# Low-rank products of a token-shift layer fed by the tokens, with two scaled sets of weights

## The chip, the cores and the metric

The kernel runs on one core of a Trainium2 chip. The metric is the device time of one execution in microseconds, from the first to the last instruction and the little around them; lower is better. Five engines share the work: PE (matrix products, with PEld for its weight loads), DVE and ACT (elementwise work, also on the accumulators of PE), POOL (elementwise work outside the accumulators) and SP, whose queue issues nearly all transfers.

## What is computed

The program is a network of three layers over 512 tokens of 1024 features, with a second stream of 256 context tokens in the first two. The change lies in layer 1, an RWKV layer. Its features start from a shift of every token to its neighbours:

```
def centred_shift(x):
    prev = jnp.pad(x[:, :-1], ((0, 0), (1, 0), (0, 0)))
    nxt = jnp.pad(x[:, 1:], ((0, 0), (0, 1), (0, 0)))
    return 0.5 * (prev + nxt) - x

def rwkv_features(h, mu, wr, wk, wv, w0, w1, w2, a0, a1, a2, g1, g2, ...):
    xx = centred_shift(h)
    mix = lambda j: h + xx * mu[j]
    xw, xk, xv, xa = mix(1), mix(2), mix(3), mix(4)
    k = xk @ wk
    v = heads(xv @ wv)
    for d in range(2):
        w_raw = heads(w0[d] + jnp.tanh(xw @ w1[d]) @ w2[d])
        a = jax.nn.sigmoid(heads(a0[d] + (xa @ a1[d]) @ a2[d]))
    r = heads(mix(0) @ wr)
    g = jax.nn.sigmoid(mix(5) @ g1) @ g2
```

`h` are the normalised and modulated tokens. Three pairs of weights are low-rank: `w1, w2` (decay), `a1, a2` and `g1, g2` (gate), with 128 inner features each once both directions `d` stand side by side. The products with `w1`, `a1`, `g1` are called the first low-rank products here, those with `w2`, `a2`, `g2` the second ones. All is fp32; the big products are split into a rounded part and a rest and done in three matmuls, the first low-rank products are done in plain fp32.

## The kernel before

Features lie on the 128 partitions (8 blocks of 128), tokens along the free axis. `features` (L1325) does the stage in question, in this order of the program:

- The six halves `lw` of the first low-rank weights are loaded (L1336) into slots of the tag `mixh`, of which there are nine.
- Layer 0's last residual sums and norms run (`residual` L688, `rms_bc` L641). For the three groups (context, first and second half of the tokens) `modulate` (L673) then makes `h` in fp32: DVE scales by the norm (L678), ACT adds the shift (L680) into `hc` (context) and `hx` (tokens), which have a zero column on either side. POOL adds the two neighbours of each token (L1352) and DVE makes `xc` and `xx` of it (L1353).
- `lora` (L1376) does a first low-rank product: for each of 8 feature blocks DVE mixes `h + xx * mu` into `mix_t` (L1382), and one matmul (L1383) accumulates it. Decay (`u` 0) and a (`u` 1) do context, then tokens in parts of 255 and 257; the gate (`u` 2) does 512 tokens at once, and comes later.
- `evac_dir` (L1386) takes the result out on ACT, turned round for the second direction, and `split` (L1390) splits it into `lr_hi` and `lr_lo`.
- `lora2` (L1395) does a second low-rank product: 16 heads, each three matmuls for 512 and three for 256 columns, an ACT tanh of each (L1405, `lr_out`), and a store. `w2bd` comes first, then the gate's first product, `a2bd`, the mixing of the operand of `wk` (`mix` L1362: DVE L1369, a cast on ACT and a subtraction on DVE in `split_sb` L594, into slots `mixh` and `mixl`), and `gates` (L1413).
- `proj` (L1460) does the product with `wk` in four units of 256 columns, each with `evac_k` (L1476) behind it: squares, norms over PE (L1487, L627) and copies turned round by POOL. Then `wr` in the same way, then `wv` together with the beginning of the scan (`Scan`, `front(0)`).

PSUM is divided into four banks `mm`, three `st` and one `a` (L1360). `st` and `a` lie where the norms of the three groups (`s0` to `s2`) lay. The order on each engine is not the program's own: a scheduler takes the instructions of the program and lays them out per engine by its own estimate of when operands are ready. An engine then does them strictly in that order. Weights of 256 columns are loaded, cast on ACT (L583, `wh`) and subtracted on DVE (L584, `wl`), two at a time (`wsplit` L578).

```
        lora2("w2bd", ts[0], hw[:, 0], self.sd, True)
        ps = self.pt("mm")
        lora(5, 2, ("x", 0, NX), ps)
...
        lora2("a2bd", ts[1], hw[:, 1], self.td, False)
        first = lambda j, wname, groups: (self.wsplit(self.i[wname][0]), mix(j, groups))
        wk = first(2, "wk", both)
        gates(tg)
...
        proj(wk, "wk", both, evac_k)
...
        proj(first(0, "wr", xo), "wr", xo, evac_r)
```

## Time and profile before

| | |
|---|---|
| median of three runs | 3165.51 us (3158.48 to 3166.71) |
| the profiled execution's own time | 3160.86 us |
| its span | 3158.9 us |
| PE busy | 2820.4 us (89%) |
| DVE busy | 1789.2 us (57%) |
| ACT busy | 1551.0 us (49%) |
| POOL busy | 1140.5 us (36%) |
| mean granted clock of PE | 0.927 of 2.4 GHz |

The table's shares are means over the whole span. The stage of the change takes some 230 us of it, from about 980 us (last norms of layer 0) to about 1210 us (begin of the product with `wr`), so it has to be read from rows of that stretch: the busy time of each engine in windows, the order of instructions in time, and what ended each wait. A granted clock of 0.50 is 1.2 GHz, 1.00 is 2.4 GHz. An fp32 matmul appears in the trace as two records, one of a split product as one.

### The profile page before, as it was taken

How to read it: one execution, taken by the hardware profiler on the slowest of the kernel's cores; microseconds unless marked ns; L12 is line 12 of the kernel's file. 1: busy time of each engine (PE TensorE's matmuls, PEld its weight loads, DVE VectorE, ACT ScalarE, POOL GpSimd, SP SyncE). 2: the span in 40 equal slices, each digit the busy share in tenths (PEclk: the TensorE clock that was granted, in tenths of full speed). 3: DMA queues.
4: the chain of work that ended last, by engine and by line, in shares of the span. 5: the costliest groups of instructions: out<-in, count | busy, mean ns of one | idle time of the engine just before them, and what ended most of it. 6: DMA issues, size and time to landing. Idle time of an engine off the chain costs nothing.

```text
span 3158.9 us, 50961 instructions
## 1 busy us (share of the span) xinstructions
PE 2820.4 (89%) x19290; PEld 2338.0 (74%) x19290; DVE 1789.2 (57%) x3558; ACT 1551.0 (49%) x3103; POOL 1140.5 (36%) x1500
## 2 busy tenths in 40 slices
PE   6999879999996899887777779699997999989999
PEld 6967778888885687764666667587776885678887
DVE  8466383444448725758688742644446654555364
ACT  3247556666664633554566532455543444544341
POOL 4013446667665212045666640256543210010000
PEclk9999989999998999987688889899998995999999
DMA  5323213333331465432233231255441220022322
GB/s 225 125 86 101 101 64 117 127 114 131 118 106 72 187 196 149 167 118 84 81 95 106 83 117 50 99 175 183 169 146 54 81 94 1 15 79 90 104 98 83
DMA packets 138115, 346.72 MB, mean 110 GB/s; under 512 B 16400, under 2 KB 48784, under 8 KB 120592
## 3 DMA queue, kind: packets, MB, share of 16 engines
q1 hardware_dynamic: 137872, 343.48, 31.8%
q8 instruction: 152, 2.49, 0.3%
q14 instruction: 91, 0.75, 0.1%
HBM read 294.40 MB, written 49.02 MB: 109 GB/s over the span
## 4 chain that ended last, share of the span: by engine, by line
PE 32%; DVE 8%; ACT 6%; POOL 6%; DMA 4%; issue 2%; SPq 0%; ACTq 0%; POOLq 0%; DVEq 0%
PE mm L590 7%; PE mm L591 7%; PE mm L592 6%; POOL acc L733 3%; DMA adaw<-in_ada_dram 3%; ACT wh L583 1%; PE st L1247 1%; PE a L329 1%; PE a L1290 1%; POOL M L428 1%; POOL Mt L427 1%; PE y L520 1%; ACT adat L732 1%; PE b L1241 1%; PE a L1924 1%
## 5 line engine op out<-in xcount | busy, mean ns | idle before, releaser
L733 POOL TENSOR_TENSOR acc<-acc,adat 128x256 f32<-128x256 f32 x658 | 575.8, 898 | 529.5 <-ACT acc L729 427.7
L584 DVE TENSOR_TENSOR wl<-wr,wh 128x2048 fp32r<-128x2048 f32 (+3 forms) x145 | 317.7, 2191 | 367.1 <-ACT wh L583 364.6
L732 ACT ACTIVATE adat<-adaw,silu 128x256 f32<-128x256 f32 x644 | 319.1, 508 | 262.1 <-POOL acc L733 161.2
L583 ACT CAST wh<-wr 128x2048 fp32r<-128x2048 f32 (+2 forms) x147 | 266.6, 1814 | 232.0 <-PE mm L591 218.1
L590 PE MATMUL mm<-fh,wh 128*128 128x512 f32 (+1 forms) x1008 | 347.3, 353 | 16.1 <-DVE relu L1015 11.7
L591 PE MATMUL mm<-fl,wh 128*128 128x512 f32 (+1 forms) x1008 | 350.8, 350 | 0.0
L592 PE MATMUL mm<-fh,wl 128*128 128x512 f32 (+1 forms) x1008 | 349.8, 349 | 0.9 <-DVE wl L584 0.9
L590 PE MATMUL mm<-h_xhi,wh 128*128 128x512 f32 (+1 forms) x784 | 278.5, 360 | 3.3 <-ACT h_xhi L596 1.9
L591 PE MATMUL mm<-h_xlo,wh 128*128 128x512 f32 (+1 forms) x784 | 277.9, 357 | 1.8 <-DVE h_xlo L686 1.5
L592 PE MATMUL mm<-h_xhi,wl 128*128 128x512 f32 (+1 forms) x784 | 277.8, 356 | 0.0
L664 POOL TENSOR_TENSOR acc<-acc,t 128x256 f32<-128x256 f32 x127 | 109.0, 866 | 345.5 <-ACT t L662 342.6
L590 PEld LDWEIGHTS mm<-fh,wh 128*128 128x128 f32 x1008 | 190.0, 189 | 43.8 <-DVE relu L1015 14.0
L592 PEld LDWEIGHTS mm<-fh,wl 128*128 128x128 f32 x1008 | 190.6, 189 | 25.5 <-DVE wl L584 1.1
L591 PEld LDWEIGHTS mm<-fl,wh 128*128 128x128 f32 x1008 | 190.7, 189 | 25.3 <-DVE fl L597 2.2
L1039 DVE TENSOR_TENSOR y<-mm,y 128x512 f32<-128x512 f32 (+1 forms) x184 | 99.2, 559 | 141.9 <-PE mm L592 141.4
L590 PE MATMUL mm<-h_hi,wh 128*128 128x512 f32 (+1 forms) x408 | 160.8, 398 | 6.7 <-ACT h_hi L685 6.7
L590 PEld LDWEIGHTS mm<-h_xhi,wh 128*128 128x128 f32 x784 | 148.0, 191 | 23.1 <-ACT h_xhi L596 2.1
L592 PEld LDWEIGHTS mm<-h_xhi,wl 128*128 128x128 f32 x784 | 148.9, 190 | 21.4 <-issue 0.2
L591 PEld LDWEIGHTS mm<-h_xlo,wh 128*128 128x128 f32 x784 | 148.9, 191 | 20.7 <-DVE h_xlo L686 1.7
L427 POOL TENSOR_TENSOR Mt<-M 128x30 f32<-128x30 f32 (+14 forms) x240 | 141.0, 588 | 56.3 <-PE f L443 21.8
L591 PE MATMUL mm<-h_lo,wh 128*128 128x512 f32 (+1 forms) x408 | 160.4, 394 | 0.0
L592 PE MATMUL mm<-h_hi,wl 128*128 128x512 f32 (+1 forms) x408 | 159.5, 393 | 0.0
(451 smaller groups left out, 6932.4 us busy)
## 6 DMA issues: line engine op xcount, KB each, us to landing
adaw<-in_ada_dram SPq DMA_DIRECT2D x256, 256.0 KB, 2.7
wr<-in_w_dram SPq DMA_DIRECT2D x64, 1024.0 KB, 4.9
wr<-in_wup_dram SPq DMA_DIRECT2D x22, 1024.0 KB, 4.8
base<-b SPq DMA_DIRECT2D x32, 384.0 KB, 3.2
ZU<-vt SPq DMA_DIRECT2D x192, 64.0 KB, 2.5
wr<-in_wdn_dram SPq DMA_DIRECT2D x16, 704.0 KB, 4.0
wr<-in_win_dram SPq DMA_DIRECT2D x9, 1024.0 KB, 4.7
wr<-in_evin_dram SPq DMA_DIRECT2D x8, 1024.0 KB, 4.8
```

Source lines behind the costliest of these rows:

```text
L329: nc.tensor.matmul(ps[:, c], bk[g][:, c0 + c].rearrange("p a t -> p (a t)"), G[:, :na, c0 + c, :], start=True, stop=True)
L427: nc.gpsimd.tensor_tensor(t, a, b, ALU.mult)
L428: nc.gpsimd.tensor_tensor(M[:, s + 1:, :s], M[:, s + 1:, :s], t, ALU.add)
L583: nc.scalar.copy(hi[:, :n], raw[:, :n])
L584: (eng or nc.vector).tensor_tensor(lo[:, :n], raw[:, :n], hi[:, :n], ALU.subtract)
L590: mm(out, lhs[0], rhs[0], start=first, stop=False)
L591: mm(out, lhs[0], rhs[1], start=False, stop=False)
L592: return mm(out, lhs[1], rhs[0], start=False, stop=last)
L664: nc.gpsimd.tensor_tensor(acc, acc, sq, ALU.add)
L732: nc.scalar.activation(t, w, AF.Copy, scale=s)
L733: nc.gpsimd.tensor_tensor(acc, acc, t, ALU.add)
L1039: nc.vector.tensor_tensor(yb, ps[:, :n], yb, ALU.add)
```

## The change

The mix is linear, so `(h + xx * mu) @ W` is `h @ ((1 - mu) W) + (left + right neighbour of h) @ (mu/2 W)`, and the second product can be made of `h` itself and its result moved by one token to either side. The change does this for the three first low-rank products.

- After the load of `lw`, two DVE instructions make `1 - mu` and `mu / 2` (`omu`), and 48 ACT instructions of 128x128 make two scaled sets of weights: `lws` (new, in six of the nine slots `mixl`) and `lw` scaled in place.
- `lora` has no mixing on DVE. For each feature block it does two matmuls on `h`, one into `pn` (scale `mu / 2`) and one into `ps` (scale `1 - mu`). The token parts are 256 and 256. `pn` takes two banks `st` for decay, one `st` and `a` for a, and one `st` for the gate.
- `both_sides` puts a result together: POOL sets two columns to zero, ACT copies `pn` into SBUF, and DVE adds it to `ps` twice, moved by one token each way. `evac_dir` reads that sum.
- The second product `a2bd` and `gates` stand behind the product with `wk` in the program, no longer ahead of it.

`xc` and `xx` are still made: the operands of `wk`, `wr` and `wv` are mixed as before.

```diff
--- before.py
+++ after.py
@@ -1334,6 +1334,16 @@
         for u in range(3):
             for k in range(2):
                 nc.sync.dma_start(lw[u * 2 + k][:, :512], self.i["lora1"][u, :, k * 512:(k + 1) * 512])
+
+        omu = mp.tile([128, 2, 48], F32, name="omu")
+        nc.vector.tensor_scalar(omu[:, 0], self.col("mu", 0, 48), -1.0, 1.0, ALU.mult, ALU.add)
+        nc.vector.tensor_scalar(omu[:, 1], self.col("mu", 0, 48), 0.5, None, ALU.mult)
+        lws = [[mp.tile([128, NT], F32, name="lws", tag="mixl", bufs=8 + 1) for _ in range(6)], lw]
+        for u, j in enumerate((1, 4, 5)):
+            for k in range(8):
+                s, f = slice(k % 4 * 128, k % 4 * 128 + 128), u * 2 + k // 4
+                nc.scalar.activation(lws[0][f][:, s], lw[f][:, s], AF.Copy, scale=omu[:, 0, j * 8 + k:j * 8 + k + 1])
+                nc.scalar.activation(lw[f][:, s], lw[f][:, s], AF.Copy, scale=omu[:, 1, j * 8 + k:j * 8 + k + 1])
         for t, n in ((hx, NX), (hc, NC_)):
             nc.gpsimd.memset(t[:, :, 0:1], 0.0)
             nc.gpsimd.memset(t[:, :, n + 1:n + 2], 0.0)
@@ -1373,19 +1383,30 @@
 
         both, xo = self.groups(), (("x", 0, NX, 0),)
 
-        def lora(j, u, part, ps):
+        def lora(j, u, part, ps, pn):
 
             g, o, n = part
-            h, d = (hc, xc) if g == "c" else (hx, xx)
+            h = hc if g == "c" else hx
             for i in range(8):
-                t = self.tmp.tile([128, 512], F32, name="mix_t", tag="t")
-                nc.vector.scalar_tensor_tensor(t[:, :n], d[:, i, o:o + n], self.col("mu", j * 8 + i), h[:, i, o + 1:o + n + 1], ALU.mult, ALU.add)
-                nc.tensor.matmul(ps[:, o:o + n], lw[u * 2 + i // 4][:, i % 4 * 128:i % 4 * 128 + 128], t[:, :n], start=i == 0, stop=i == 7)
-
-
-        def evac_dir(dst, ps, o, n, func):
-            nc.scalar.activation(dst[0:64, o:o + n], ps[0:64, :n], func)
-            nc.scalar.activation(dst[64:128, o:o + n][:, ::-1], ps[64:128, :n], func)
+                s, f = slice(i % 4 * 128, i % 4 * 128 + 128), i // 4
+                for p, q in ((pn, 1), (ps, 0)):
+                    nc.tensor.matmul(p[:, o:o + n], lws[q][u * 2 + f][:, s], h[:, i, o + 1:o + n + 1], start=i == 0, stop=i == 7)
+
+        def both_sides(ps, pn, n, t, o):
+
+            b = self.tmp.tile([128, 516], F32, name="lr_n", tag="lr_n", bufs=2)
+            nc.gpsimd.memset(b[:, 0:1], 0.0)
+            nc.gpsimd.memset(b[:, n + 1:n + 2], 0.0)
+            nc.scalar.copy(b[:, 1:n + 1], pn[:, :n])
+            nc.vector.tensor_tensor(t[:, o:o + n], ps[:, :n], b[:, 0:n], ALU.add)
+            nc.vector.tensor_tensor(t[:, o:o + n], t[:, o:o + n], b[:, 2:n + 2], ALU.add)
+
+
+        def evac_dir(dst, ps, pn, o, n, func):
+            t = self.tmp.tile([128, 512], F32, name="lr_s", tag="t")
+            both_sides(ps, pn, n, t, 0)
+            nc.scalar.activation(dst[0:64, o:o + n], t[0:64, :n], func)
+            nc.scalar.activation(dst[64:128, o:o + n][:, ::-1], t[64:128, :n], func)
 
         def split(t, n):
             hi, lo = (lp.tile([128, NT], F32R, name=k, tag=k, bufs=2) for k in ("lr_hi", "lr_lo"))
@@ -1422,27 +1443,27 @@
                 nc.sync.dma_start(self.gd[s, :], u[:, :NX])
 
         both_lora = ((1, 0, AF.Tanh), (4, 1, AF.Copy))
-        pss = [(self.pt("mm"), self.pt("mm")) for _ in both_lora]
-        for part in parts:
+        pss = [[self.pt(t) for t in tags] for tags in (("mm", "mm", "st", "st"), ("mm", "mm", "st", "a"))]
+        for part in (("c", 0, NC_), ("x", 0, 256), ("x", 256, 256)):
             for (j, u, _), ps in zip(both_lora, pss):
-                lora(j, u, part, ps[part[0] == "x"])
+                x = part[0] == "x"
+                lora(j, u, part, ps[x], ps[2 + x])
         ts = []
         for (_, _, func), ps in zip(both_lora, pss):
             t = p2.tile([128, NT], F32, name="lr", tag="rev")
-            evac_dir(t, ps[0], 0, NC_, func)
-            evac_dir(t, ps[1], NC_, NX, func)
+            evac_dir(t, ps[0], ps[2], 0, NC_, func)
+            evac_dir(t, ps[1], ps[3], NC_, NX, func)
             ts.append(split(t, NT))
         lora2("w2bd", ts[0], hw[:, 0], self.sd, True)
-        ps = self.pt("mm")
-        lora(5, 2, ("x", 0, NX), ps)
+        ps, pn = self.pt("mm"), self.pt("st")
+        lora(5, 2, ("x", 0, NX), ps, pn)
         t = p2.tile([128, NT], F32, name="lr", tag="rev")
-        nc.scalar.activation(t[:, :NX], ps, AF.Tanh, scale=0.5)
+        both_sides(ps, pn, NX, t, 0)
+        nc.scalar.activation(t[:, :NX], t[:, :NX], AF.Tanh, scale=0.5)
         nc.vector.tensor_scalar(t[:, :NX], t[:, :NX], 0.5, 0.5, ALU.mult, ALU.add)
         tg = split(t, NX)
-        lora2("a2bd", ts[1], hw[:, 1], self.td, False)
         first = lambda j, wname, groups: (self.wsplit(self.i[wname][0]), mix(j, groups))
         wk = first(2, "wk", both)
-        gates(tg)
 
         def rev(src, n, b, fwd, bwd):
 
@@ -1495,6 +1516,8 @@
             rev(kk, NT, b, self.b0, self.b1)
 
         proj(wk, "wk", both, evac_k)
+        lora2("a2bd", ts[1], hw[:, 1], self.td, False)
+        gates(tg)
 
         def evac_r(b, pss):
             t = p2.tile([128, NT], F32, name="rblk", tag="kblk")
```

On ACT, in the last norms of layer 0, ahead of the first `hc`. `acc` and `t` are the squares of `rms_bc` (L649 and L662), `lws` and `lw` the two sets of weights. Before:

```order
L662 ACTIVATE acc<-x 128x256
L649 ACTIVATE t<-y 128x256 x2
L608 ACTIVATE rs_t<-rms_v 128x2
L662 ACTIVATE t<-x 128x256
L653 ACTIVATE t<-t 128x256
L662 ACTIVATE t<-x 128x256 x6
L649 ACTIVATE t<-x 128x256 x2
L608 ACTIVATE rs_t<-rms_v 128x2
```

In the changed kernel:

```order
L662 ACTIVATE acc<-x 128x256
L1345 ACTIVATE lws<-lw,omu 128x128 x2
L649 ACTIVATE t<-y 128x256
L1345 ACTIVATE lws<-lw,omu 128x128 x2
L1346 ACTIVATE lw<-lw,omu 128x128
L649 ACTIVATE t<-y 128x256
L1345 ACTIVATE lws<-lw,omu 128x128 x2
L1346 ACTIVATE lw<-lw,omu 128x128
L1345 ACTIVATE lws<-lw,omu 128x128 x2
L1346 ACTIVATE lw<-lw,omu 128x128
L1345 ACTIVATE lws<-lw,omu 128x128 x4
L1346 ACTIVATE lw<-lw,omu 128x128
```

All 48 scalings stand between the squares of the norms, ahead of the first `hc`.

On ACT, in the second product `w2bd`. `lr_out` is the tanh of a head, `mixh` the cast of the operand of `wk`. Before (the rows alternate like this for all of `w2bd`):

```order
L1405 ACTIVATE lr_out<-mm,hw 128x256
L1405 ACTIVATE lr_out<-mm,hw 128x512
L583 CAST wh<-wr 128x2048
L1405 ACTIVATE lr_out<-mm,hw 128x256
L1405 ACTIVATE lr_out<-mm,hw 128x512
```

In the changed kernel:

```order
L1400 COPY lr_n<-st 128x512
L596 CAST mixh<-mix_t 128x512
L1426 ACTIVATE lr_out<-mm,hw 128x512
L1426 ACTIVATE lr_out<-mm,hw 128x256
L596 CAST mixh<-mix_t 128x256
L1426 ACTIVATE lr_out<-mm,hw 128x512
L1426 ACTIVATE lr_out<-mm,hw 128x256
L596 CAST mixh<-mix_t 128x512
L596 CAST mixh<-mix_t 128x256
```

The casts of `wk`'s operand, which stood between the heads of `a2bd`, now stand between those of `w2bd`.

On PE, at the end of the product with `wk`. `st<-cst,rb` and `st<-cst,sq` are the norms of `evac_k`, `lr_hi` and `lr_lo` the operand of a second low-rank product. Before:

```order
L592 MATMUL mm<-mixh,wl 128x512
L1487 MATMUL st<-cst,sq 128x2 x4
L627 MATMUL st<-cst,rb 128x128 x6
L1487 MATMUL st<-cst,sq 128x2 x6
L627 MATMUL st<-cst,rb 128x128 x6
L590 MATMUL mm<-mixh,wh 128x512 x4
```

In the changed kernel:

```order
L592 MATMUL mm<-mixh,wl 128x512
L590 MATMUL mm<-lr_hi,wh 128x512
L591 MATMUL mm<-lr_lo,wh 128x512
L592 MATMUL mm<-lr_hi,wl 128x512
L1508 MATMUL st<-cst,sq 128x2 x4
L590 MATMUL mm<-lr_hi,wh 128x256
L591 MATMUL mm<-lr_lo,wh 128x256
L592 MATMUL mm<-lr_hi,wl 128x256
L627 MATMUL st<-cst,rb 128x128 x2
```

Before, the last norms of `wk` stood alone ahead of `wr`; now the heads of `a2bd` and the gates stand between them and ahead of `wr`.

## Rows read from the trace of the kernel before

**Rows 1.** Windows: stretch, its length, busy time (instructions) per engine, clock, DMA, GB/s.

```profile
1010.00:1020.00 10.00, 0.00 (x0) 0.00 (x0) 10.00 (x21) 3.35 (x8) 5.69 (x8) 0.65 0.00 0
1020.00:1030.00 10.00, 1.21 (x3) 1.02 (x4) 9.82 (x28) 7.41 (x11) 6.69 (x9) 0.50 0.60 220
...
1040.00:1050.00 10.00, 10.00 (x47) 7.43 (x46) 9.73 (x23) 1.30 (x4) 0.00 (x0) 0.99 0.00 0
...
1060.00:1070.00 10.00, 9.39 (x53) 7.93 (x52) 1.46 (x2) 9.96 (x21) 6.75 (x9) 1.00 0.76 295
```

**Rows 2.** Windows of 2 us in the last norms, and after them.

```profile
1004.00:1006.00 2.00, 1.90 (x5) 0.95 (x4) 2.00 (x7) 1.61 (x5) 1.95 (x4) 0.50 0.94 393
1006.00:1008.00 2.00, 1.17 (x7) 1.12 (x8) 2.00 (x7) 1.55 (x4) 1.11 (x3) 0.96 0.93 393
...
1034.00:1036.00 2.00, 1.45 (x4) 0.50 (x2) 2.00 (x2) 0.00 (x0) 0.00 (x0) 0.50 0.88 328
```

**Rows 3.** PE in order of time: start, length, instruction, count [idle before].

```profile
1007.38 1.46 PE L650 MATMUL s<-t,cst 128*128 128x256 f32 x6
1028.79 2.90 PE L1383 MATMUL mm<-mix_t,lw 128*128 128x256 f32 x6 [19.95 <-issue]
...
1056.13 0.94 PE L590 MATMUL mm<-lr_hi,wh 128*128 128x512 f32 x3
...
1075.14 2.74 PE L1383 MATMUL mm<-mix_t,lw 128*128 128x512 f32 x6
```

**Rows 4.** ACT in order of time, in the last norms.

```profile
1000.64 0.42 ACT L649 ACTIVATE t<-x 128x256 f32<-128x256 f32 x1 [6.82 <-POOL x L693]
...
1002.56 0.89 ACT L680 ACTIVATE hc<-t,mod 128x256 f32<-128x256 f32 x2
```

**Rows 5.** ACT in order of time: a scaling of layer 0's weights and a small copy.

```profile
936.85 0.50 ACT L732 ACTIVATE adat<-adaw,silu 128x256 f32<-128x256 f32 x1
937.26 0.39 ACT L596 CAST fh<-relu 128x256 fp32r<-128x256 f32 x1
...
1290.70 0.26 ACT L335 COPY Ld<-a 32x128 f32<-32x128 f32 x1
```

**Rows 6.** ACT in order of time, in the second low-rank products.

```profile
1062.74 12.98 ACT L1405 ACTIVATE lr_out<-mm,hw 128x512 f32<-128x512 f32 x25
1075.62 1.89 ACT L583 CAST wh<-wr 128x2048 fp32r<-128x2048 f32 x1
...
1094.51 0.48 ACT L596 CAST mixh<-mix_t 128x256 fp32r<-128x256 f32 x1
1094.81 0.78 ACT L1405 ACTIVATE lr_out<-mm,hw 128x512 f32<-128x512 f32 x1
1095.39 0.70 ACT L596 CAST mixh<-mix_t 128x512 fp32r<-128x512 f32 x1
1095.90 0.57 ACT L1405 ACTIVATE lr_out<-mm,hw 128x256 f32<-128x256 f32 x1
```

**Rows 7.** PE in order of time: gates, begin and end of `wk`, begin of `wr`.

```profile
1106.15 0.50 PE L590 MATMUL mm<-lr_hi,wh 128*128 128x512 f32 x1 [1.50 <-ACT wh L583]
...
1112.07 0.28 PE L590 MATMUL mm<-mixh,wh 128*128 128x256 f32 x1
...
1195.67 0.95 PE L1487 MATMUL st<-cst,sq 128*128 128x2 f32 x8
1201.12 2.90 PE L627 MATMUL st<-cst,rb 128*128 128x128 f32 x12 [4.50 <-DVE rb L623]
...
1209.37 1.89 PE L590 MATMUL mm<-mixh,wh 128*128 128x512 f32 x4
```

**Rows 8.** ACT in order of time, in `evac_k`.

```profile
1131.73 1.28 ACT L608 ACT_TABLE_LOAD   x1
...
1202.35 0.69 ACT L1484 ACTIVATE sq<-mm,cols 128x512 f32<-128x512 f32 x1 [3.82 <-PE st L627]
```

**Rows 9.** The chain of waits from 1290 us on, one of its longest pieces.

```profile
1881.50 8.14 DMA ZU<-vt
```

## Prediction

> **What bounds the kernel now.** I read the busy time in windows first, to find the engine that sets the pace of each part of the stage, then the instructions of PE and ACT in order of time, to put lengths on the parts, and the waits beside them.
>
> Four parts follow each other. From 1008.8 to 1028.8 PE has nothing to do and DVE is busy without a gap, with the modulation and the shifts [rows 1]; the first product starts at 1028.79 after 19.95 us of idleness [rows 3]. From 1040 on it is PE that bounds: 47 records in 10.00 us, 0.213 us each, at the upper clock level [rows 1]. An fp32 product of 256 columns, two records, so takes 0.426 us, and one of 512 columns 0.853 (six records in 2.74 us less the last one's tail, 0.427 each [rows 3]). So the DVE mixing that the change removes was not the limit where the first products ran; it only kept PE from starting. The second products begin at 1056.13 [rows 3] and are paced by ACT: 9.96 of 10 us busy with the tanh of `w2bd` alone [rows 1], 25 of them in 12.98 us, 0.52 each [rows 6]. With `a2bd` the casts of `wk`'s operand come in between. The gates begin at 1106.15, `wk` at 1112.07; PE does nothing else until 1196.6, waits 4.50 us and more for the last norms, and `wr` begins at 1209.37 [rows 7]. From there on the change alters nothing but the order that the scheduler finds, so I count to the begin of `wr`.
>
> **Part 1, up to the begin of `w2bd`.** DVE loses 56 mixes, which lay beside PE's products from 1040 on and cost nothing there. PE gains as many products as it had: 96 instead of 48 of 256 columns, 96 x 0.426 = 40.9 us, and 16 instead of 8 of 512. It can start when the first `hc` is there, at 1002.56 plus its half microsecond before [rows 4]. But the 48 scalings stand ahead of it on ACT. A scaling of 256 columns by a column of SBUF holds ACT 0.41 us, from 936.85 to 937.26 [rows 5]; 128 columns less I put at 0.31, so 14.7 us together. ACT's other work in the last norms is some 5.4 us, and it had one gap of 6.82 us there [rows 4]. From 984.8, with 1 us until the first weights land and 1 us for waits on POOL's sums, the first `hc` begins at about 1006.4 instead of 1002.56. Bounds: 0.26 us per scaling, a small copy, and everything in gaps, which delays nothing; 0.41 each, as for 256 columns [rows 5], which adds 4.9 us.
>
> From the first `hc` at 1006.9 I take PE as saturated: 40.9 us, eight norm products (six records in 1.46 us [rows 3], so 3.9 for sixteen), 0.7 for two small ones, 6.0 for seven of the gate's `pn` products, which the scheduler puts ahead of `w2bd`, and 2 us because the clock begins at 0.50. It rose to 0.96 between 1006 and 1008 after PE had been 1.90 of 2 us busy [rows 2]; I price the same start, about 4 us at half pace. That is 53.5 us: `w2bd` begins at 1060.4, 4.3 later than before. The new evacuation (a copy of 0.6, two DVE additions, two tanh, a cast, a subtraction, some 5 us) lies under the 14 products of `a` and 7 of the gate, 12.0 us; were that cover gone it would cost its 5. Ten POOL memsets and two DVE instructions on `omu` are off the path, under 0.1 us each.
>
> **Part 2, up to the begin of `wk`.** Before 55.9 us (1056.13 to 1112.07), with `a2bd` and gates in it. Now: 2.8 us until the first tanh (the last `pn` product 0.9, its copy, one cast), then ACT's stream of 32 tanh x 0.52 = 16.6, five casts of 256 columns (0.30 from start to start) and five of 512 (0.51 [rows 6]), 4.1, and one of a weight, 1.8: 22.5. PE's last product is some 1.8 ahead of ACT's last tanh. Then eight `ps` products of the gate, 6.8. Sum 2.8 + 22.5 - 1.8 + 6.8 = 30.3, 25.6 less than before. Lower bound: `w2bd` at its old length, 1056.13 to 1075.14 [rows 3], 19.0 + 6.8 = 25.8. Upper: 34, if ACT waits for DVE as well. The cast slots: the last `mixl` reuses a slot that the gate's `ps` weights hold until PE has passed them, but it is needed 14 us into `wk`; no cost. The gate's own evacuation lies under `wk`, which needs its bank 1.4 us in, after one addition of 0.7.
>
> **Part 3, `wk`,** stays at 84.5 us. The loads of `a2bd` and `g2w` move behind stores on SP's queue, but are issued tens of microseconds ahead of use; the third and fourth loads of `wr` come behind the stores of `td`, which delays nothing that PE needs within 10 us.
>
> **Part 4, from the last product of `wk` to `wr`.** Before 12.8 us (1196.6 to 1209.37). Now `a2bd` and gates lie here. ACT must first do the last square, which waited for PE until 1202.35 [rows 8]; the weights split on DVE ahead of it are half as long, so I put its end at 4.3 us. Then the tanh and the square root alternate: three table loads of 1.28 [rows 8], two tanh, one root, 5.1. Then 30 tanh 15.6, casts for `wr` 4.9, one weight 1.8: 22.3. Minus PE's lead 1.7, plus the gates, 5.9 as from 1106.15 to 1112.07 [rows 7]. Sum 35.9, 23.1 more. Lower bound: PE alone, heads at 1.05 us and gates, 22.8. Upper: 42, if `lr_out` waits for the stores of `wk`'s last blocks, whose buffers it takes over.
>
> The price of a table load is where page and trace differ. The row has 1.28 us, and the load at 1131.73 begins 0.02 us after ACT's previous instruction ends [rows 8]. The Trainium skill, "ScalarE: Activation LUTs", section "What ACT_TABLE_LOAD costs", counts about 2.66 us for every switch, with a drain; by that the three would cost 4.1 us more and the sum would be +5.9. The trace shows no drain ahead of a load, so I keep the row.
>
> **The sum** is +4.3 - 25.6 + 0 + 23.1 = +1.8 us: the doubled products and the tanh moved behind `wk` take back what an earlier start gives. The profiled execution took 3160.86, so 3162.7 against it. The median of the runs shown is 4.65 above; I set the level between the two, 3163.2, and forecast **3165 us**. A difference of 0.3%, 9.5 us, is about what a measurement of this kernel can tell from none.
>
> **Rivals.** (A) *Faster: ACT does not pace.* If the scalings fit in ACT's gaps (part 1 +0.3), `w2bd` keeps its old length (25.8) and `a2bd` behind `wk` runs at the same 19.0 plus 5.9 for the gates plus 2.6 for tables (27.5, +14.7), the sum is +0.3 - 30.1 + 14.7 = -15, so 3148. For it: the exposed 4.50 us and the cold norms ahead of `wr` [rows 7] are exactly what `a2bd` fills. Against: ACT was 9.96 of 10 busy with tanh alone [rows 1]. Partly true (-11) it still counts as faster. Chance 0.24.
>
> (B) *Slower: the clock stays at its lower level while `hc` and `hx` come in.* The new products depend on tokens that ACT and DVE deliver one block at a time. If these gaps hold the clock at 0.50 until the last `hx`, at about 1028, PE does half as much in 17 more us, 8.5 us lost: +10.3, 3173. It decides when PE does not reach 0.9 before about 1020. For it: from 1034 to 1036 PE was 1.45 of 2 us busy in pieces and the clock stayed at 0.50; against: at 1.90 of 2 it had risen [rows 2], and four products per block keep it fuller than one did. The Trainium skill, "TensorE: Matmul & The Clock Gate", section "HAM oscillation — how this bites in real kernels", tells of loops in which each wait for data sends the clock back to its lower level; by that rule this rival's time holds. Chance 0.15.
>
> (C) *The order behind the stage.* The scheduler lays out the scan anew after any change, and its chain has single exposed transfers of up to 8.14 us [rows 9]. One more of them gives +9.9, 3173 (chance 0.13); two fewer give -14, 3149 (0.06). Nothing in the rows says which.
>
> **Chances and range.** The forecast, within 9.5 us either way, has 0.42. Faster 0.30 (A 0.24, C 0.06), slower 0.28 (B 0.15, C 0.13). The range reaches to A and C below, 3148, and to B with a scaling at its upper bound above, 3180; about one in ten lies beyond either end.
>
> **What would show it.** After the change the first low-rank product should start near 1007, PE be full from there to about 1060 with the clock up by 1012; `w2bd` begin near 1060, `wk` near 1091, its last product near 1175, `wr` near 1211. ACT should be full from 986 to 1006 and through both second products. I am wrong if `hc` begins before 1004, if `a2bd` and gates take under 30 us, if the clock is low at 1020, or if `wr` begins on time and the difference lies in the scan.

## The result and the profile after

| | before | after |
|---|---|---|
| median of 7 runs each | 3166.71 us | 3185.41 us (3174.66 to 3191.93) |
| span of the profiled execution | 3158.9 us | 3183.6 us |
| mean granted clock of PE | 0.927 | 0.922 |

The ratio is 1.0063 (95% interval 1.0045 to 1.0080): 19 us slower, where 3165 was forecast and 3180 was the upper end of the range. The page of the changed kernel, busy time of each engine:

```profile
PE 2858.7 (90%) x19402; PEld 2374.5 (75%) x19402; DVE 1769.8 (56%) x3513; ACT 1567.6 (49%) x3159; POOL 1133.5 (36%) x1510
```

PE has 38 us more to do, DVE 19 less, ACT 17 more. The instructions ahead of the stage are the same in both kernels, yet layer 0's last norms begin at 964.17 in one profile and at 967.17 in the other, so I count from there. I cut both profiles at the same places: the first product of these norms, the begin of `w2bd`, of `wk`, of `wr`, the scan's first norm of an output (L530), the begin of layer 1's MLP, its last product, the first and the last product of layer 2's attention. Windows of the kernel before (columns as in [rows 1]):

```profile
964.17:1056.13 91.96, 56.77 (x307) 45.91 (x305) 83.98 (x200) 35.31 (x78) 42.71 (x62) 0.78 0.22 82
1056.13:1112.07 55.94, 51.85 (x238) 38.34 (x237) 30.71 (x48) 46.95 (x94) 15.20 (x16) 1.00 0.71 265
1112.07:1209.37 97.30, 91.00 (x577) 82.68 (x576) 33.94 (x79) 28.70 (x50) 14.16 (x30) 0.97 0.63 192
1209.37:1502.47 293.10, 242.14 (x1971) 194.12 (x1970) 202.33 (x381) 147.41 (x301) 96.37 (x152) 0.87 0.39 123
...
2032.97:2410.38 377.41, 362.67 (x1783) 302.24 (x1784) 185.76 (x261) 195.86 (x331) 173.06 (x176) 1.00 0.44 151
...
2598.62:2741.12 142.50, 138.37 (x653) 79.22 (x652) 74.73 (x340) 73.94 (x207) 0.00 (x0) 0.73 0.03 11
```

The same stretches of the changed kernel:

```profile
967.17:1062.01 94.84, 79.23 (x420) 68.03 (x419) 71.61 (x171) 53.97 (x137) 42.93 (x72) 0.91 0.23 85
1062.01:1092.28 30.27, 27.16 (x117) 18.59 (x115) 20.31 (x27) 23.65 (x47) 16.28 (x16) 1.00 0.50 199
1092.28:1218.30 126.02, 118.86 (x698) 103.73 (x697) 49.75 (x104) 55.23 (x99) 15.80 (x32) 0.96 0.61 196
1218.30:1515.34 297.04, 245.85 (x1986) 197.31 (x1984) 192.65 (x362) 145.64 (x302) 98.61 (x159) 0.86 0.41 130
...
2046.96:2430.21 383.25, 367.32 (x1783) 305.60 (x1784) 186.21 (x261) 196.21 (x331) 171.70 (x176) 0.99 0.44 149
...
2618.82:2766.35 147.53, 140.65 (x653) 81.29 (x652) 73.76 (x339) 73.70 (x208) 0.00 (x0) 0.73 0.03 11
```

The stage, the first three rows of each, is 251.1 us long instead of 245.2: 5.9 more. Behind `wr`, where not one instruction was edited, the beginning of the scan costs 3.9 more, the MLP 5.8, the attention 5.0. So less than a third of what was lost lies where the prediction looked. These are lengths of one profile each; how far they repeat, the runs below show.

Inside the stage the first product answers to [rows 3], and the windows to [rows 1]. PE in order of time, then two windows of the changed kernel:

```profile
1010.56 1.91 PE L1393 MATMUL mm<-hc,lws 128*128 128x256 f32 x4
```

```profile
1010.00:1020.00 10.00, 10.00 (x42) 8.50 (x42) 6.90 (x21) 4.58 (x13) 4.20 (x6) 0.84 0.32 133
1020.00:1030.00 10.00, 10.00 (x48) 8.75 (x47) 9.90 (x21) 3.35 (x9) 5.32 (x8) 1.00 0.00 1
```

PE is full where it stood idle, with the clock at its upper level from 1020 on. The stretch between the last product of `wk`, at 1176.5, and `wr` answers to [rows 8]. ACT in order of time:

```profile
1181.68 0.69 ACT L1505 ACTIVATE sq<-mm,cols 128x512 f32<-128x512 f32 x1 [2.21 <-PE st L627]
1185.19 1.28 ACT L1426 ACT_TABLE_LOAD   x1 [2.81 <-DVE kkblk L1514]
1186.48 1.05 ACT L1426 ACTIVATE lr_out<-mm,hw 128x512 f32<-128x512 f32 x2
1187.55 1.28 ACT L608 ACT_TABLE_LOAD   x1
1188.85 0.21 ACT L608 ACTIVATE rs_t<-kkv 128x12 f32<-128x12 f32 x1
1190.75 1.28 ACT L1426 ACT_TABLE_LOAD   x1 [1.69 <-DMA b<-kkblk]
1192.04 1.05 ACT L1426 ACTIVATE lr_out<-mm,hw 128x512 f32<-128x512 f32 x2
```

The first tanh of `a2bd` waits 2.81 us for the buffer that `kkblk` is still made from, the third 1.69 us for the store of another of `wk`'s blocks, and three tables are loaded in between.

### The profile page after: what moved, and what is told of

Its sections match the earlier page's. It is cut to its first block, busy times and chain, and to the rows that moved or that the text cites. A ratio compares the mean times of both kernels' runs of the same rounds, so it can differ in the third digit from the quotient of the medians.

```text
span 3183.6 us, 51203 instructions
## 1 busy us (share of the span) xinstructions
PE 2858.7 (90%) x19402; PEld 2374.5 (75%) x19402; DVE 1769.8 (56%) x3513; ACT 1567.6 (49%) x3159; POOL 1133.5 (36%) x1510
```

## The experiments

**How an order is held.** The scheduler lays out every engine anew after an edit. To test the order by itself, most of these kernels bind each instruction behind some point of the program to its predecessor on its engine in another kernel's order. This adds no wait; a table of numbers (`order`, one list per engine) comes from the other kernel, and the copies whose engine the scheduler would choose (`nc.any`) keep that kernel's engine.

```diff
+def pin(tc):
+    traced = [i for b in tc._region_blocks() for i in b.instructions][-N:]
+    for q in order.values():
+        for a, b in zip(q, q[1:]):
+            tc.add_manual_dep(traced[b], traced[a].name, info, reason="order")
...
         Prog(tc, ins, out).run()
+        pin(tc)
```

All lengths are in us, from the profile of each run; "held" is the order of before or after that the program keeps, and from where. Stage is from the last norms to `wr`, scan from `wr` to its first norm. Every ratio is to the kernel before, timed beside the run on the same chip.

| run | held | ratio (95%) | stage | scan | MLP | attention |
|---|---|---|---|---|---|---|
| before | | 1 | 245.2 | 293.1 | 377.4 | 142.5 |
| e5, before again | own | 1.0014 (0.9993 to 1.0035) | 245.4 | 295.5 | 378.6 | 125.9 |
| after | | 1.0063 (1.0045 to 1.0080) | 251.1 | 297.0 | 383.2 | 147.5 |
| e9, after again | own | 1.0064 (1.0047 to 1.0080) | 251.2 | 298.8 | 383.3 | 145.9 |
| e1, after | before, `wr` | 1.0049 (1.0037 to 1.0062) | 254.1 | 296.9 | 379.9 | 142.8 |
| e10, after | before, `wv` | 1.0036 (1.0024 to 1.0048) | 251.6 | 293.8 | 379.2 | 139.6 |
| e6, after | before, MLP | 1.0066 (1.0040 to 1.0091) | 250.4 | 299.4 | 380.7 | 142.4 |
| e2, before | after, `wr` | 1.0092 (1.0076 to 1.0109) | 254.3 | 302.1 | 383.5 | 147.4 |
| e7, before | after, MLP | 1.0036 (1.0018 to 1.0053) | 247.5 | 295.0 | 383.5 | 140.3 |
| e3, doubled products | before, `wr` | 1.0033 (1.0021 to 1.0045) | 248.9 | 296.1 | 380.0 | 142.6 |
| e4, move | before, `wr` | 1.0027 (1.0018 to 1.0036) | 250.4 | 297.4 | 377.4 | 142.5 |
| e8, decay | before, MLP | 1.0073 (1.0047 to 1.0098) | 243.1 | 310.0 | 378.8 | 142.9 |
| e11, decay | before, `wv` | 1.0010 (0.9999 to 1.0021) | 244.1 | 294.7 | 379.1 | 139.7 |
| e12, after, relieved | before, `wv` | 1.0003 (0.9987 to 1.0019) | 247.1 | 294.8 | 379.0 | 125.9 |
| e13, decay and move | before, `wv` | 0.9977 (0.9964 to 0.9991) | 238.4 | 290.4 | 377.6 | 142.5 |
| e14, move, relieved | before, `wv` | 0.9984 (0.9966 to 1.0001) | 241.7 | 292.3 | 376.9 | 139.5 |

**e1 and e2: the orders exchanged from `wr` on.** The edit is `pin` alone, with the other kernel's table.

> The changed kernel, with every instruction from the first load of wr's weights on held, on each engine, to the order that it has in the kernel before. Measured so far: the change costs 20 us of 3167 (ratio 1.0063); in the two traces wr begins 5.9 us later once the 3.0 us by which the last norms already start late are taken off, and the rest, some 14 us, comes behind wr. Theory ORDER (the rest comes from the order that the scheduler found behind wr): with the old order only the stage's 6 us remain, ratio 1.002. Theory STAGE (the order is worth nothing; what comes later is what the late second products and their stores delay, whatever the order): the ratio stays at 1.006.

> The mirror image: the kernel before, with everything from the first load of wr's weights on held to the order that it has in the changed kernel. Theory ORDER: about 14 us slower than before although the stage is the old one, ratio 1.0045. Theory STAGE: as fast as before, ratio 1.000 within 0.2%.

e1, 1.0049, came out between the two theories, with STAGE's 1.006 inside its interval, and e2, 1.0092, beyond both. The table says why. Held from `wr` on, an order meets a stage that it was not made for: PE waits ahead of `wr`, and the stage grows by 3 us in e1 and 9 in e2. Behind that, though, the MLP goes with the order and not with the stage: it takes 379.9 with the old one and 383.5 with the new. The scan's beginning grows in e2, to 302.1, but does not shrink in e1 (296.9 against 297.0).

**e3 and e4: one half of the change each.** In e3 `a2bd` and the gates go back ahead of `wk`; in e4 the first products are the old ones and only this move is made (the edit of e4 against before, without `pin`):

```diff
-        lora2("a2bd", ts[1], hw[:, 1], self.td, False)
         first = lambda j, wname, groups: (self.wsplit(self.i[wname][0]), mix(j, groups))
         wk = first(2, "wk", both)
-        gates(tg)
...
         proj(wk, "wk", both, evac_k)
+        lora2("a2bd", ts[1], hw[:, 1], self.td, False)
+        gates(tg)
```

> The doubled first products alone: a2bd and the gates stay ahead of wk, and everything from wr on is held to the order of the kernel before. From the traces: w2bd begins 5.9 us later in the changed kernel, 3.0 of it there before the stage began, so about 3 us; from w2bd to wr ACT paces as before. Theory ORDER: 3 us slower, ratio 1.001, wr 3 us late. Theory STAGE: the late a2bd is what delays, so with a2bd ahead of wk nothing is left but those 3 us: also 1.001. If the doubled products are what costs most, 1.003 or more.

> The move alone: the first products mixed on DVE as before, a2bd and the gates behind wk, and everything from wr on held to the order of the kernel before. From the traces: w2bd to wk 24.9 us shorter, last product of wk to wr 28 longer (12.8 before, some 41 after), so 3 us late at wr. Theory ORDER: 3 us slower, ratio 1.001. Theory STAGE: most of the 20 us lie here, ratio 1.005.

Both halves cost: 1.0033 and 1.0027 where ORDER had 1.001 for each. The doubled products alone bring `wr` 3.7 us late where 3 were expected, and their ratio lies above the 1.003 that was named as the mark for "what costs most"; the move alone brings it 5.2 late, with part of that due to the held order as in e1, where it was 3. The two intervals overlap, so which half costs more is not shown. Nor do most of the 20 us lie in the move, as STAGE had it: 1.005 was expected there.

**e5: the kernel before once more.**

> The kernel before once more, to see by how much two profiles of one program differ (it is held to its own order, which changes no instruction). Ratio 1.000. In the four runs so far the last norms of layer 0 began 964 to 973 us into the span although nothing ahead of them differs, so this one should lie between these; from there to wr 245.2 us again, within 0.3. The product part of layer 1's MLP took 377.4 us in two runs with the old order and 380 in two others, with two short falls of the clock more; if that is chance this run shows 377 to 381.

The stage repeats to 0.2 us here (in e7 below, the same instructions in the same order took 2.3 us more, so a difference of 2 us between two single profiles shows little) and the MLP lies in the range named. The attention does not repeat: its clock came back 38 us sooner than in the first profile (shown in the last section). A length there proves nothing about a kernel from one profile.

**e6 and e7: the orders exchanged from layer 1's MLP on.** Again `pin` alone, so that the stage and the scan are those of the kernel itself.

> The changed kernel, untouched up to layer 1's MLP, and held to the order of the kernel before only from that MLP on. Theory TAIL: the new order costs 5.0 us in layer 2's attention (147.5 us from the first to the last of its products in both runs with the new order, 142.6 in the four with the old one) and 3 to 6 in the MLP (383.2 and 383.5 against 377.4 to 380.0). Then attention takes 142.6, the MLP 377 to 380, and the whole is 8 to 11 us faster than the changed kernel: ratio to before 1.003. Rival CHANCE: those two parts were long by how the clock happened to fall: attention and MLP as long as in the changed kernel, ratio 1.006.

> The kernel before, untouched up to layer 1's MLP, and held to the order of the changed kernel from there on. Theory TAIL: attention 147.5 us, MLP 383, 8 to 11 us slower than before, ratio 1.003, with not one instruction of the stage changed. Rival CHANCE: attention 142.6, ratio 1.000.

Windows of MLP and attention, first of e6, then of e7:

```profile
2053.01:2433.71 380.70, 365.76 (x1783) 304.77 (x1784) 185.95 (x261) 195.79 (x331) 173.20 (x176) 0.99 0.44 150
...
2622.03:2764.48 142.45, 138.37 (x653) 79.27 (x652) 74.72 (x340) 74.00 (x207) 0.00 (x0) 0.73 0.03 11
```

```profile
2045.70:2429.18 383.48, 367.55 (x1783) 306.01 (x1784) 186.11 (x261) 196.41 (x331) 171.82 (x176) 0.99 0.44 149
...
2617.78:2758.11 140.33, 133.28 (x653) 77.36 (x652) 73.73 (x339) 73.52 (x208) 0.00 (x0) 0.77 0.03 11
```

e7 is 0.36% slower although its stage is the old one, as TAIL had it (by the medians, 3172.20 against 3164.86, it is 7.3 us), and the MLP takes 383.2 to 383.5 in all four profiles with the new order, 376.9 to 380.7 in the twelve others. The attention is half a miss: PE's idle time there is 7.05 us in e7 (140.33 less 133.28) and 4.08 in e6; it is 6.6 to 7.1 in the four profiles with the new order and 4.1 to 5.3 in the twelve others, so some 2 us are the order's; the rest of the 5 was the clock. e6's two segments shrank about as expected, but its ratio did not: 1.0066 is what CHANCE had. Its scan was longer, in the profile at least, and the interval is 0.5% wide. Of the two mirror images one bears TAIL out and the other does not.

One place where the order of the MLP tells can be read. ACT of the changed kernel, then PE of the changed kernel, then ACT of the kernel before, at the same step:

```profile
2072.47 1.89 ACT L583 CAST wh<-wr 128x2048 fp32r<-128x2048 f32 x1
2074.26 0.40 ACT L596 CAST fh<-relu 128x256 fp32r<-128x256 f32 x1
```

```profile
2073.16 0.40 PE L592 MATMUL mm<-fh,wl 128*128 128x512 f32 x1
2074.72 0.73 PE L590 MATMUL mm<-fh,wh 128*128 128x512 f32 x2 [1.16 <-ACT fh L596]
2077.61 0.50 PE L591 MATMUL mm<-fl,wh 128*128 128x512 f32 x1 [2.16 <-DVE fl L597]
...
2078.61 0.63 PE L592 MATMUL mm<-fh,wl 128*128 128x512 f32 x1
```

```profile
2059.24 0.39 ACT L596 CAST fh<-relu 128x256 fp32r<-128x256 f32 x1
2059.54 1.91 ACT L583 CAST wh<-wr 128x2048 fp32r<-128x2048 f32 x1
```

A weight cast of 1.9 us changed places with the cast of `fh` that PE needs at once. On DVE the subtraction for that weight changed places with the subtraction that makes `fl`:

```profile
2074.39 2.29 DVE L584 TENSOR_TENSOR wl<-wr,wh 128x2048 fp32r<-128x2048 f32 x1 [2.09 <-ACT wh L583]
2076.60 0.95 DVE L597 TENSOR_TENSOR fl<-relu,fh 128x256 fp32r<-128x256 f32 x1
```

PE waits 1.16 and 2.16 us, and the products after it take 0.63 instead of 0.40: the granted clock had fallen to 0.50.

**e8: doubled products for decay alone.** `w2bd` needs only decay, so its products go first; `a` and the gate are mixed as before, behind `w2bd` in the program:

```diff
-        for u, j in enumerate((1, 4, 5)):
+        for u, j in ((0, 1),):
...
+        for part in (("c", 0, NC_), ("x", 0, 256), ("x", 256, 256)):
+            lora(1, 0, part, ps[part[0] == "x"], ps[2 + (part[0] == "x")])
...
         lora2("w2bd", t, hw[:, 0], self.sd, True)
+        for part in parts:
+            lora_mix(4, 1, part, ps[part[0] == "x"])
...
+        lora_mix(5, 2, ("x", 0, NX), ps)
...
+        lora2("a2bd", ta, hw[:, 1], self.td, False)
```

> Doubled products for decay alone, whose second product w2bd is what comes next; a and the gate are mixed on DVE as before, and their first products follow w2bd in the program; a2bd and the gates stay ahead of wk. Only 16 scalings instead of 48 stand ahead of hc on ACT (some 5 us instead of 15). From layer 1's MLP on the order is that of the kernel before. Theory: in the changed kernel 53 us of products keep PE full up to w2bd, so doubling all three fills the time that the earlier start gives; of decay alone 20 us are done when the last hx comes in, about 64 us after the last norms' begin, so w2bd starts at 70 to 75 us from there instead of 92, ACT goes through both second products at 0.52 a tanh beside DVE's mixing of a, and wk begins some 20 us earlier than before: ratio 0.994. Rival: DVE, full with modulation and shifts up to that point, delays the evacuation and the mixing of a, so that w2bd begins no earlier than 84 and a2bd waits: 5 us or less are won, ratio 0.998 or more.

`w2bd` begins 80.7 us after the last norms, between the two theories. `wk` begins hardly sooner than before, as the rival had it, but not because of DVE: PE is busy 59.2 of the 64.9 us in between, with `w2bd`, `a2bd` and the products that now lie there. The stage wins 2.1 us, and the scan's beginning loses 17.

**e9 to e12: the order by itself, and the stretch ahead of `wr`.** e9 is the changed kernel again, e10 the same with the old order from `wv` on, e11 is e8 with the old order from `wv` on. e12 is e10 with two edits more:

```diff
-                u = p2.tile([128, NT], F32, name="lr_out", tag=("kblk", "kkblk", "rev")[h % 3])
+                u = p2.tile([128, NT], F32, name="lr_out", tag=("kblk", "kkblk", "rev")[h % 3]) if sigmoid else lp.tile([128, NT], F32, name="lr_out", tag="lr_out", bufs=4)
...
-            r = self.rsqrt_small(v, 12)
+            r = self.rsqrt_small(v, 12, sqrt=False)
```

> The changed kernel once more (held to its own order, which changes no instruction), beside the next one. Ratio 1.006. From the last norms to wr 251 us, wr to the scan's first norm of an output 297 to 299.5, the MLP 383, attention 147 or less where the clock happens to be higher.

> The changed kernel, untouched through wr, and held to the order of the kernel before from the product with wv on (the first of these runs held wr as well, and PE then waited 5 us ahead of wr for weights in an order that was not made for this stage). Theory ORDER, now with sizes by segment: stage +5.6 us against before, wr to the scan's first norm 294.5 to 296 as in the old order instead of 297 to 299.5, MLP 377 to 380 instead of 383, attention 142.6 instead of 147.5: 9 to 11 us faster than the changed kernel in the same call, ratio to before 1.003. Rival: the second run of the old tail saved 7.6 us in its two segments and still was not faster in the median; if order is worth nothing in sum, the two kernels of this call differ by under 4 us.

> Doubled products for decay alone, as in the eighth run, there 243.2 us from the last norms to wr against 245.2 before, but 153 us instead of 137 to 138.5 from the end of wv to the scan's first norm, and 1.0073 in all. Now held to the order of the kernel before from wv on, no longer from the MLP on alone. Theory ORDER: those 15 us are the order of the scan's beginning; they go, that stretch takes 137 to 139, and the kernel is 2 us faster than before or level: ratio 0.999. Rival STAGE: the products that now come in w2bd's time delay stores or loads that the scan's beginning needs: the stretch stays above 145 us, ratio 1.005.

> The changed kernel with its stretch from the last product of wk to wr relieved: a2bd's lr_out has four buffers of its own instead of those of wk's blocks, and the norms of evac_k take their square root on DVE, so that ACT loads no table between tanh and root. From wv on in the order of the kernel before. In the changed kernel the stretch takes 41.8 us, 5.9 more than I had worked out; ACT waits there 2.81 and 1.69 us for buffers and loads three tables of 1.28. Theory BUFFERS: without these 8.3 us it takes 33 to 35, wr begins 243 us after the last norms, 2 before its old time, and the whole is level with the kernel before: ratio 0.998 to 1.001. Rival CHAIN: the norms of wk's last two blocks, which go round PE, DVE and PE, set the end: 39 or more, ratio 1.003.

ORDER holds. e10's median is 3179.60 us, e9's, timed beside it on the same chip, 3191.66: 12 us, or 9 by the two ratios, by nothing but the order behind `wr`. Every run of e10 (3177 to 3183) is below every run of e9 (3184 to 3194). The scan's beginning takes 297.0 to 302.1 with the new order; with the old one it takes 290.4 to 295.5 (e10 293.8), or 296.1 to 297.4 where that is held from `wr` on. e11 shows it once more, windows from `wr` to the scan's first norm in e8 and in e11:

```profile
1210.37:1520.32 309.95, 251.40 (x2048) 200.53 (x2048) 203.61 (x390) 154.83 (x326) 104.92 (x171) 0.85 0.37 116
```

```profile
1214.45:1509.14 294.69, 242.36 (x1970) 193.21 (x1970) 201.57 (x381) 147.51 (x301) 95.61 (x152) 0.86 0.38 121
```

The 15 us go with the order, and the kernel from 1.0073 to 1.0010. (The windows end at an event that comes at another place in another order, hence the other counts.)

e12 is level with before, 1.0003, as BUFFERS said, but not for its reason: from `wk` to `wr` it takes 122.1 us, 3.9 less than the changed kernel and not the 7 to 9 named, and the stretch behind the last product of `wk` takes some 39.5, a length that CHAIN had named. What sets it is not CHAIN's norms, though, but ACT's stream of tanh. SP's queue and ACT in this stretch of e12:

```profile
1184.08 3.42 SPq L1479 DMA_DIRECT2D b<-rev  x4
1187.60 2.43 SPq L1429 DMA_DIRECT2D td<-lr_out  x3
```

```profile
1191.94 2.94 ACT L1426 ACTIVATE lr_out<-mm,hw 128x512 f32<-128x512 f32 x6 [3.56 <-DMA td<-lr_out]
```

The first tanh is now at 1181.03, but the first store of an `lr_out` is issued at 1187.60, behind eight of `wk`'s blocks on SP's queue; the four buffers run full, and a wait of 3.56 us took the place of those removed. Part of its ratio is luck as well: its profile, of the run of 3158.22 us, has the short attention, 125.9; three of its twelve runs lie at 3157 to 3159, and by the medians (3173.98 against 3168.72) it is 5 us slower than before.

**e13 and e14: does doubling give anything at all?** e13 is e11 with the move and the relief of e12; e14 is e4 with that relief, held from `wv` on. (The expectation of e13 says 72 added products; they are 56, 48 of 256 columns and 8 of 512, and their 27 us stand.)

> Decay alone with doubled products (w2bd begins 80.2 us after the last norms instead of 94.6), a2bd and the gates behind wk with the relief of the twelfth run (122.1 us from wk to wr instead of 126), old order from wv on. Theory PE WORK: the change does not pay in its stage because the 72 added products are 27 us of PE, which fill the 20 us that PE stood idle; with 24 of them, 10 us, the early start is kept: w2bd to wk is 33 us of products (19 of w2bd, 7 of a, 7 of the gate) and some 3 of waits, so wk begins 116 us and wr 238 us after the last norms instead of 245.3 before: 7 us faster, ratio 0.998. Rival ACT OR DVE: the evacuation and the mixing of a, the gate and wk's operand do not get done in 36 us, w2bd to wk takes 43 or more: level with before, 1.000.

> No doubled products at all: the first products mixed on DVE as before, and only a2bd and the gates moved behind wk, with the relief of the twelfth run; old order from wv on. Theory PE WORK: 92.0 us to w2bd as before, 27.4 from there to wk and 122.1 from wk to wr: 241.5 against 245.3, 4 us faster, ratio 0.999, and 3 us slower than the thirteenth run. Rival: what made the stretch from wk to wr shorter in the twelfth run was the earlier start; then it takes 126 or more here and the kernel is level with before.

Windows of the stage, first of e13, then of e14:

```profile
969.09:1049.21 80.12, 59.25 (x322) 49.68 (x321) 69.41 (x166) 39.85 (x94) 42.93 (x66) 0.87 0.27 101
1049.21:1083.03 33.82, 31.75 (x150) 24.49 (x149) 22.94 (x30) 22.00 (x40) 14.53 (x16) 1.00 0.44 176
1083.03:1207.44 124.41, 118.12 (x696) 103.19 (x697) 73.59 (x181) 56.51 (x103) 23.32 (x33) 0.96 0.61 199
```

```profile
972.73:1064.36 91.63, 57.65 (x306) 46.45 (x305) 83.45 (x200) 35.34 (x78) 42.92 (x62) 0.78 0.24 88
1064.36:1091.81 27.45, 25.14 (x118) 18.57 (x117) 11.85 (x15) 20.27 (x37) 15.19 (x16) 1.00 0.64 238
1091.81:1214.44 122.63, 115.99 (x698) 101.39 (x697) 72.59 (x181) 57.03 (x103) 20.89 (x32) 0.99 0.61 197
```

Stages of 238.4 and 241.7 us against 238 and 241.5 worked out, and ratios of 0.9977 and 0.9984 against 0.998 and 0.999: PE WORK holds in the stage (in e13 by two errors of 2 us that cancel: `wk` began 114 us after the last norms and not 116, and 124.4 us passed from there to `wr`, not 122.1). With 24 of the 56 added products the early start is kept. One rival is that fewer scalings stand ahead of `hc` on ACT, 16 instead of 48. The traces speak against it: the first `hc` begins 40.3 us after the last norms in e13 and 40.8 in the changed kernel (38.4 before), half a microsecond apart, while `w2bd` begins 14.7 apart; and from the first product to `w2bd` PE is busy 51.5 of 51.5 us in the changed kernel, 30.3 of 38.2 in e13. In the whole time e13 and e14 cannot be told apart (3162.45 and 3162.99). e13 is faster than the kernel before by 0.23% (0.09 to 0.36), which is under the 0.3% that the prediction took for tellable.

## Why the prediction was wrong

**Part 1 was right to 1.4 us.** `w2bd` was to come 4.3 us late. Counted from the last norms it came 2.9 late (94.84 against 91.96), and 94.5 to 95.1 in all seven profiles with this stage's beginning. A scaling takes 0.29 to 0.30 from one start to the next (four of them from 994.02 to 995.19) where 0.31 was taken, and the 48 delayed the first `hc` by 2.4 us where 3.8 stood. The first product came at 1010.56 instead of 1006.9, 3.0 of it because the norms began later.

**Part 2 was exact in length:** 30.3 predicted, 30.27 measured, a little of it by luck. The weight's cast of 1.8 us, which the sum has in ACT's stream, came at 1086.27, when PE was through with `w2bd`; waits of ACT for DVE's mixing, 1.3 us in all, took its place. Part 3 was unchanged to 0.6 us: 84.2 from 1092.28 to 1176.49, where before it was 83.6 by the same mark (the 84.5 ran on to the end of the squares behind the last product).

**Part 4 is the term that was mis-sized:** 35.9 predicted, 41.8 measured, with 42 named as the upper bound for just this reason. By its own steps: the first table load was to come 4.3 us after the last product of `wk` and came 8.7 after it, 1.6 because the last square ended late and 2.8 because `lr_out` takes over `wk`'s buffers; the switches were to take 5.1 and took 6.8, with a wait of 1.69 for a store; the 30 tanh with the casts took 22.5 where 22.3 stood. So I had named the wait and then chosen the value without it. e12, which takes it away, won 3.9 us and found the next wait behind it.

The price of a table load was right: three times 1.28, with the next instruction 1.29 or 1.30 us after each load's start. The Trainium skill, "ScalarE: Activation LUTs", section "What ACT_TABLE_LOAD costs", has the same 1.28 for the load and adds a drain of 1.38. Behind these loads there is no room for one, and the load at 1187.55 begins 0.02 us behind ACT's last tanh; ahead of the other two ACT was idle, 2.81 and 1.69 us, which the trace puts down to buffers. That the prediction's sum with the price of the Trainium skill, +5.9, is also what the stage measured is chance.

**The step that failed** is the sentence that from `wr` on the change alters nothing but the order, "so I count to the begin of `wr`". The order alone is worth more than the stage: 9 to 12 us between e9 and e10, and 7 to 11 more than before for e7, whose stage is untouched (the smaller and the larger of what ratios and medians give). That is about half of the loss, and it stood at nothing in the sum. Rival C had the right place, and too small a chance and price: I gave it one exposed transfer of the chain [rows 9]. What it cost lies elsewhere: 4 us in the beginning of the scan, 4 to 6 in the MLP, where a weight cast stands ahead of a cast that PE waits for, and some 2 of idle PE in the attention, up to 1500 us behind the edit. With 5.9 for the stage that is 16 to 18, from single profiles; measured were 18.7 in the medians.

**Rival A** fell: ACT did pace (from 1065 to 1085 it is busy 18.69 of 20.00 us, PE 16.89). Its 3148 needed a stage 15 us shorter; the best of these runs, e13, is 7 shorter. **Rival B** fell: the clock was at 1.00 from 1020 on. The Trainium skill, "TensorE: Matmul & The Clock Gate", section "HAM oscillation — how this bites in real kernels", expects the lower level where products wait for data one after the other. Here two products for each block of `hc` as it came in, with the norms' own products between them, kept PE at 10.00 of 10 us from 1010 on already (the other two for each block came from 1036.51 on), so its case did not arise.

**Where the expected gain went.** Counted from the last norms PE began the first products 21 us earlier than before (43.4 against 64.6), and had 27 us more to do (48 products of 0.426 and 8 of 0.853). That was in the sum, and lengths of the stage show it: doubling all three products costs 3.7 us (e3) or 5.3 (e12, 247.1, against e14, 241.7), doubling the one that is needed first gives 3.3 (e13 against e14).

**Still open:** e10, with the old order, is 11 us (8 to 15) above before, while its stage explains 6, and e6 gained nothing by the old order of MLP and attention; e10's scan behind the first norm was 3 us longer than before's, and the scan of unchanged programs varied by as much (531.6 and 537.1 us from its first norm to the MLP in the two profiles of the changed kernel). Nor was it traced which instruction makes the scan's beginning longer in the new order.

## What to carry to other kernels

Where a scheduler lays out the whole program, an edit has two effects: what it does in its stage, and a new order everywhere behind it. Hold the order behind the edit and time both ways before judging the edit; here that was worth more than the stage itself. Moving work from an idle engine's neighbour onto it pays only as far as the idle time reaches: here, in lengths of the stage, it paid to double the one product that the next step waits for, and cost to double all of them. And a step that is moved behind another inherits that one's buffers and its stores' place in the queue: price those waits, not only the instructions.

## What the runs showed of the hardware

The clock can stay at its lower level while PE has hardly a gap in the rows (where the ends of products are modelled). Attention of the kernel before, windows of 5 us, 35, 75 and 80 us after its begin, and then of the same program in e5, 35, 40 and 45 us after it:

```profile
2633.60:2638.60 5.00, 5.00 (x16) 2.75 (x16) 3.36 (x16) 2.58 (x8) 0.00 (x0) 0.50 0.00 2
...
2673.60:2678.60 5.00, 5.00 (x15) 2.63 (x15) 2.75 (x12) 1.54 (x4) 0.00 (x0) 0.50 0.00 0
2678.60:2683.60 5.00, 5.00 (x34) 3.04 (x32) 3.67 (x17) 3.80 (x11) 0.00 (x0) 0.99 0.00 0
```

```profile
2643.50:2648.50 5.00, 5.00 (x15) 2.75 (x16) 3.47 (x16) 2.70 (x8) 0.00 (x0) 0.50 0.01 2
2648.50:2653.50 5.00, 5.00 (x24) 2.98 (x23) 2.47 (x16) 2.82 (x9) 0.00 (x0) 0.78 0.00 0
2653.50:2658.50 5.00, 5.00 (x31) 2.82 (x30) 3.03 (x17) 3.32 (x10) 0.00 (x0) 1.00 0.02 3
```

The same instructions, PE at 5.00 of 5 us in both, and the rise came 38 us apart, counted from the begin of the attention: 142.5 us for the attention or 125.9, 16.6 us and so nearly the whole effect of this change, by the clock alone. What decides it is open. In the same way equal pauses of PE in the MLP were followed by the lower level in some profiles and not in others: 2.54 us, 123 us into the MLP, by a granted clock of 1.00 in the kernel before (window 2158 to 2163), and 2.42 us at the same place by 0.66 in e13 (same window). And the stretch ahead of the last norms, the same instructions in every kernel, took 964 to 973 us.
